# Two-layer diffusion block on one core: seventeen expert loads ahead of the routing, ranks beside the gather, down weights in 8 KB runs

## The chip, the cores and the metric

The kernel runs on one core of a Trainium2 chip. The metric is the device time of one execution in microseconds, as the median of several runs; lower is better. TensorE is called PE here (its weight loads PEld), VectorE DVE, ScalarE ACT, GpSimd POOL, and SyncE SP. SP computes nothing: it issues the loads from device memory (HBM) into the on-chip memory, in the order of its program.

## The reference

Two layers work on 256 latent tokens of width 1024. The first mixes by pooling and latent attention and has a dense SwiGLU. The second mixes by a Hyena convolution and then has a mixture of eight experts of hidden width 3584, of which each token takes two. Everything is float32. The change lies at and behind the routing of the second layer, which is this:

```python
def moe_swiglu(h, router_w, wg, wu, wd):
    t = h.reshape(-1, shp[-1])
    logits = (t @ router_w).astype(jnp.float32)
    top_v, top_i = lax.top_k(logits, TOP_K)
    gates = jax.nn.softmax(top_v, axis=-1)
    combine = jnp.sum(jax.nn.one_hot(top_i, N_EXPERTS) * gates[..., None], axis=1)
    out = jnp.zeros_like(t)
    for e in range(N_EXPERTS):
        out = out + combine[:, e:e + 1] * swiglu(t, wg[e], wu[e], wd[e])

def swiglu(h, wg, wu, wd):
    return (jax.nn.silu(h @ wg) * (h @ wu)) @ wd
```

The weights of all eight experts are read once: 3 x 8 x 1024 x 3584 numbers of 4 bytes, 352 MB.

## The kernel before

**The stages.** Layer one, then the Hyena mixer, whose last step is the output product with `hy_out_w` (keys `ho`, four row blocks). Then come the residual and layer norm of each half of the tokens (tb 0 and 1), the router's logits, and the routing on DVE: `top` twice, a one-hot `mask` of the two experts of each token, and on PE a product with a triangular matrix that gives each token its place among its expert's tokens (`posm`). Then the tokens of expert 0 are gathered by matmuls with one-hot matrices (`gather_open`, `gather_block`), and the experts run.

**The experts.** Slot 0 is expert 0; the other slots are the experts in the order of their token counts, which `weights()` computes on DVE (`key`, `rank`, `pick`, `ids`, and by them `poss` and `combs`). So an address of slot 1 to 7 is known only when SP has read the number from `ids` (`expert`, L179). Slots 0 to 4 have room for 96 tokens (three strips of 32; called H here), slots 5 to 7 for 64 (L). A strip of 32 tokens is the stationary operand, so one expert matmul (L1329) multiplies 32 columns by 256 and four of them share the array. Each slot's 3584 hidden features are cut into four tiles of 1024, 1024, 1024 and 512 (`TILES`); slot and tile make a step, and `STEPS` orders the 32 steps as HH LHHLH LHHLH ... HLHHL.

**A step.** Step i does `up` (gate and up products), `hidden` (silu and product), then the `down` of step i-1, then `turn`: the hidden block, 256 features wide, is transposed by PE in two halves of 128, features 0 to 127 and 128 to 255. In steps 0 and 1 the gather of the next unit of slots follows.

**The loads.** Every expert load is 1 MB in one of a set of 8 KB-per-partition buffers. A step of 1024 features has eight gate and up loads and four down loads, one of 512 features four and two; in all 336 loads, which are numbered from 0 here. A gate or up load is 256 rows by 1024 columns, so runs of 4 KB (2 KB in tiles of 512). A down load is 256 full rows of 4 KB; partition p gets rows p and p + 128 (`"(k p) n -> p k n"`). Loads 0 to 19 are of expert 0 and need no number.

**The buffers.** `wp` holds four `raw`, three `whi` and three `wlo` buffers, which the earlier stages use too: the `ho` rows are split into `whi` and `wlo` parts. When the pools of the Hyena stage close, `mr` (five) and `mt` (two) open in their place. `W(key)` issues the loads up to `depth` ahead of the one asked for. Before the routing it is called with depth NRAW + 1 = 5, when only the four `raw` buffers are there, so load 4 takes the buffer of load 0; then with depth 17. `mt` goes after step 0, so that 15 buffers turn round from then on. `load` chains each load behind the one before; the read of a number at L179 is not in that chain.

**Around it.** `sub_lo(nl, ...)` on POOL makes the low part of the normed tokens. `busy` gives PE idle transposes, 8 and 24 of them, behind each half's logits. `gather_block` takes its result out by ACT and DVE in turn. `carry` (four POOL operations on `h`) waits for `st["late"]`, a small copy behind the last block of the gather.

Of the kernel before, what the change touches and what calls it, by code (L numbers as in the profile page):

```python
# [8 lines left out]
F32 = mybir.dt.float32  # L9
# [8 lines left out]
P = 128  # L18
T = 256
# [41 lines left out]
def block_kernel(ctx: ExitStack, tc: tile.TileContext, A, dbg=None):  # L61
# [50 lines left out]
    def fetch(i):  # L112
        e = plan[i]
        if callable(e[0]):
            e[0] = e[0]().rearrange("(k p) n -> p k n", p=P)
        if e[2] == "place":
            load(e[1]() if callable(e[1]) else e[1], e[0])
            return
        k = e[0].shape[1]
        r = raw_tile(e[4])[:, :k * e[1]].rearrange("p (k n) -> p k n", k=k)  # L120
        load(r, e[0])
        e[3] = r
# [51 lines left out]
    def expert(nm, e):  # L174

        if e == 0:
            return A[nm][0, 0]
        if e not in number:
            number[e] = nc.values_load(st["ids"][0:1, e:e + 1], engines=(mybir.EngineType.SP,), min_val=0, max_val=NE - 1)  # L179
        return A[nm][0][bass.ds(number[e], 1)].rearrange("a k f -> (a k) f")  # L180
# [79 lines left out]
    def want_rest():  # L260
# [34 lines left out]
        def rows_of(nm, e, r, n, c0, w):  # L295

            return lambda: expert(nm, e)[r:r + n, c0:c0 + w]

# [654 lines left out]
    with ExitStack() as ctx2:  # L953
# [89 lines left out]
        with tc.tile_pool(name="hy", bufs=1) as hy:  # L1043
# [126 lines left out]
            dump("mh", yh.bitcast(F32))  # L1170
            st["ahead"], st["depth"] = 0, NRAW + 1
            out_rows(ys, [("ho", r) for r in (2, 3)], [pairs(yh, yl, r) for r in (2, 3)], False, True)
# [8 lines left out]
        mt = late.enter_context(tc.tile_pool(name="mt", bufs=1, side="right"))  # L1181
        extra["me"] = [[(mt, NMT, "raw"), (mr, NME, "raw"), (wp, NRAW, "raw"), (wp, NHL, "whi"), (wp, NHL, "wlo")], -1]
        st["depth"] = NRAW + NME + NMT + 2 * NHL
# [18 lines left out]
        with tc.high_priority():  # L1202
            for tb in range(2):
                residual(ln, ys, t, gates[1, 2], tb)
                for i in range(2):
                    ps = bank()
                    with tc.issue_after(st["out"].ins):
                        for j in range(4):
                            k = 4 * i + j
                            PE.transpose(ps[:, j * P:(j + 1) * P], t[:, tb, k * P:(k + 1) * P], ident)  # L1210
                    zcopy = S.copy(zT[:, tb, 4 * i:4 * i + 4, :], ps.rearrange("p (j n) -> p j n", j=4))
                pl = bank()[:, :NE]
                for k in range(KB):
                    last = PE.matmul(pl, zT[:, tb, k, :], arw[:, k, :], start=k == 0, stop=k == 7)
                sums.append((pl,) + norm(t, tb, h))
                busy((8, 24)[tb], last)
            for tb in range(2):
# [3 lines left out]
                with tc.issue_after(sums[1][3].ins):  # L1221
                    V.tensor_scalar(nr, r, -1.0, None, op0=ALU.mult)
                    V.scalar_tensor_tensor(u, rsum[:, 0, :], m, pl, op0=ALU.mult, op1=ALU.subtract)
                    V.scalar_tensor_tensor(lg[:, tb, :], u, nr, rsum[:, 1, :], op0=ALU.mult, op1=ALU.add)
        st["first"] = st["stat"]
        for tb in range(2):
            with tc.issue_after(zcopy.ins):
                S.copy(nh[:, tb, :], h[:, tb, :])
            st["late"] = sub_lo(nl[:, tb, :], h[:, tb, :], nh[:, tb, :], G)

# [24 lines left out]
        top(lg2, m2, i2, oh2)  # L1255
        st["next"] = V.tensor_tensor(mask, oh1, oh2, op=ALU.add)
        pq = bank()[:, :24]
        pp_ = pq[:, :16].rearrange("p (b e) -> p b e", e=NE)
        tri = cst[:, C_TRI:C_TRI + P]
        PE.matmul(pp_[:, 0, :], tri, mask[:, 0, :], start=True, stop=True)  # L1260
        PE.matmul(pp_[:, 1, :], tri, mask[:, 1, :], start=True, stop=False)
        PE.matmul(pp_[:, 1, :], cst[:, C_ONE:C_ONE + P], mask[:, 0, :], start=False, stop=True)
        V.scalar_tensor_tensor(posm, pp_, 1.0, mask, op0=ALU.add, op1=ALU.mult)
        st["ahead"], st["cut"] = 1, 2
        W(("mg", 0, 0, 0))
# [8 lines left out]
    with tc.tile_pool(name="my", bufs=1) as my, tc.tile_pool(name="me", bufs=1) as me, late:  # L1274
# [100 lines left out]
        def turn(e, f, hid):  # L1375

            hT = []
            for s, t in enumerate(hid):
                n = t.shape[0]
                ps = mbank("ms")[:, :256].rearrange("p (q n) -> p q n", q=2)  # L1380
                for q in range(2):
                    PE.transpose(ps[:, q, :n], t[:, q * P:(q + 1) * P], ident[:n, :n])  # L1382
                x = me.tile([P, 2, P], F32, tag="hT", name="hT", bufs=8)
# [68 lines left out]

        V.tensor_tensor(ex, m2, m1, op=ALU.subtract)
        S.activation(ex, ex, AF.Exp)
        gather_open(0, posm)
        ring = extra["me"]
        for k in range(KB):
            gather_block(0, k, k % 2 == 0)
        done = small.tile([P, 1], F32, tag="done", name="done", bufs=1)
        st["late"] = G.tensor_copy(done, unit[0][1][:, KB - 1, 0:1])  # L1460
        carry(h, g, b)


# [7 lines left out]
        pick, prod = sm([NE, NE], "pick"), sm([NE, NE], "prod")  # L1471
        more = sm([2, NE], "more", I32)

        def by_rank(dst, x):

            V.tensor_tensor(prod, pick, x.unsqueeze(1).to_broadcast(wide), op=ALU.mult)
            V.tensor_reduce(dst, prod, axis=AX.X, op=ALU.add)

        def weights():

            V.tensor_scalar(r1, ex, 1.0, None, op0=ALU.add)
            V.reciprocal(r1, r1)
# [3 lines left out]
            V.tensor_tensor(comb, oh1, oh2, op=ALU.add)  # L1486
            pc = mbank("ms")[:, :NE]
            for tb in range(2):
                PE.matmul(pc, ones, mask[:, tb, :], start=tb == 0, stop=tb == 1)
            V.scalar_tensor_tensor(key, pc, float(-NE), iota8, op0=ALU.mult, op1=ALU.add)  # L1490
            V.memset(key[:, 0:1], -1e6)
            V.tensor_tensor(prod, key.unsqueeze(2).to_broadcast(wide), key.unsqueeze(1).to_broadcast(wide), op=ALU.is_gt)
            V.tensor_reduce(rank, prod, axis=AX.X, op=ALU.add)
            V.tensor_scalar(rank, rank, float(-NE), None, op0=ALU.add)
            V.tensor_tensor(pick, iota8.unsqueeze(2).to_broadcast(wide), rank.unsqueeze(1).to_broadcast(wide), op=ALU.is_equal)
            idf = sm([NE], "idf")
            st["ids"] = sm([NE], "ids", I32)
            by_rank(idf, iota8)
            V.tensor_scalar(st["ids"], idf, float(NE), None, op0=ALU.add)
            for tb in range(2):  # L1500
                by_rank(poss[:, tb, :], posm[:, tb, :])
                by_rank(combs[:, tb, :], comb[:, tb, :])
# [6 lines left out]
            mosti = small.tile([P, 1], I32, tag="r_mosti", name="mosti", bufs=1)  # L1509
            V.tensor_tensor(idf, pc, slots, op=ALU.subtract)  # L1510
            V.tensor_reduce(most, idf, axis=AX.X, op=ALU.max)
# [4 lines left out]
            dump("posm", posm)  # L1516
            return mosti

        NF2 = len(TILES)
# [110 lines left out]
        load(lnb, A["ln_b"][1, 1:2, :].to_broadcast([P, D]))  # L1630
        v = nc.values_load(mosti[0:1, 0:1], min_val=0, max_val=T)
        for n in range(2):
# [111 lines left out]
```

## Time and profile before

| what | us |
|---|---|
| median of three runs (lowest, highest) | 1488.97 (1487.72, 1490.21) |
| the profiled execution, its own time | 1491.33 |
| its span, first to last instruction | 1489.6 |
| PE busy | 1395.9 |
| DVE busy | 532.5 |
| ACT busy | 318.6 |
| POOL busy | 74.6 |
| DMA traffic | 485.88 MB |

The busy time of PE counts overlapping matmuls that wait for one another as busy, so it doesn't tell how much faster PE could go; the distance from one group of matmuls to the next does. The page cuts the span into 40 slices of 37.2 us and gives for each the rate of the DMA engines in GB/s.

### The profile page before, as it was taken

The numbers are of one execution on the slowest core, as the hardware profiler recorded it, in microseconds if no ns is written. First come the engines' busy times: TensorE is split into PE (matmuls) and PEld (weight loads), VectorE is DVE, ScalarE is ACT, GpSimd is POOL, SyncE is SP. The second block draws the span as 40 slices with busy tenths as digits, with TensorE's granted clock in tenths as the row PEclk, the third lists the DMA queues.
The fourth block names the chain that finished last, engine by engine and source line by source line (L and its number), as shares of the span: only waits on it lengthen the run. The fifth ranks groups of instructions, "written<-read, shape, count | busy, mean of one in ns | idle before, by whom it ended". The sixth has DMA issues, their size and how long they took to land. (4 is left out here: it accounts for less than half of the span.)

```text
span 1489.6 us, 39345 instructions
## 1 busy us (share of the span) xinstructions
PE 1395.9 (94%) x17906; PEld 943.1 (63%) x17907; DVE 532.5 (36%) x889; ACT 318.6 (21%) x515; POOL 74.6 (5%) x68
## 2 busy tenths in 40 slices
PE   6899998999989997999999999999899999999994
PEld 3676778999979885565555555555465555455552
DVE  5656788886588765100110002200002110110005
ACT  2546643334344430100000011000010000000000
POOL 1300011000020203000000000000000000000000
PEclk9999998999999997999999999999999999999997
DMA  9965798897562622999999999999999999999992
GB/s 295 327 233 170 258 351 292 299 312 268 184 201 69 237 89 109 408 408 401 407 407 408 407 390 407 408 408 407 399 387 400 408 407 384 408 408 408 389 389 99
DMA packets 179888, 485.88 MB, mean 326 GB/s; under 512 B 8829, under 2 KB 49981, under 8 KB 179645
## 3 DMA queue, kind: packets, MB, share of 16 engines
q1 hardware_dynamic: 178112, 479.97, 84.9%
q10 hardware_dynamic: 1598, 3.27, 0.7%
q8 instruction: 144, 2.36, 0.7%
q14 instruction: 34, 0.28, 0.1%
HBM read 480.06 MB, written 3.15 MB: 324 GB/s over the span
## 5 line engine op out<-in xcount | busy, mean ns | idle before, releaser
L1329 PE MATMUL up<-raw,xt 128*32 128x256 f32 x9408 | 536.7, 382 | 21.4 <-DMA raw<-in_moe_gate_dram 11.0
L1329 PEld LDWEIGHTS up<-raw,xt 128*32 128x32 f32 x9408 | 303.5, 110 | 236.7 <-DMA raw<-in_moe_up_dram 20.0
L1366 DVE TENSOR_TENSOR sg<-up,sg 128x256 f32<-128x256 f32 (+1 forms) x71 | 30.0, 423 | 545.8 <-ACT sg L1364 545.5
L1329 PE MATMUL ac<-raw,hT 128*32 128x256 f32 x3360 | 192.0, 380 | 0.5 <-DMA raw<-in_moe_down_dram 0.5
L160 PE MATMUL mm<-zl,whi 128*128 128x256 f32 x544 | 155.5, 286 | 4.3 <-DVE zl L164 4.3
L159 PE MATMUL mm<-zh,whi 128*128 128x256 f32 x544 | 155.7, 289 | 1.0 <-DVE m L1106 1.0
L135 DVE TENSOR_TENSOR wlo<-raw,whi 128x2048 fp32r<-128x2048 f32 (+4 forms) x63 | 137.9, 2192 | 51.4 <-ACT whi L131 51.3
L161 PE MATMUL mm<-zh,wlo 128*128 128x256 f32 x544 | 153.5, 284 | 0.0
L1329 PEld LDWEIGHTS ac<-raw,hT 128*32 128x32 f32 x3360 | 107.6, 110 | 72.1 <-issue 2.7
L1364 ACT ACTIVATE sg<-up 128x256 f32<-128x256 f32 (+1 forms) x76 | 28.6, 382 | 576.2 <-PE up L1329 574.3
L131 ACT CAST whi<-raw 128x2048 fp32r<-128x2048 f32 (+3 forms) x61 | 113.1, 1854 | 151.7 <-PE mm L160 84.7
L160 PEld LDWEIGHTS mm<-zl,whi 128*128 128x128 f32 x544 | 104.8, 193 | 7.4 <-DVE zl L164 5.9
L159 PEld LDWEIGHTS mm<-zh,whi 128*128 128x128 f32 x544 | 104.3, 193 | 4.3 <-ACT zh L887 1.7
L161 PEld LDWEIGHTS mm<-zh,wlo 128*128 128x128 f32 x544 | 104.4, 192 | 0.5 <-issue 0.5
L1329 PE MATMUL al<-raw,hT 128*32 128x256 f32 x1344 | 80.7, 381 | 3.0 <-DVE hT L1387 2.1
L842 POOL TENSOR_TENSOR v<-v,mhalf 128x1 f32<-128x1 f32 x8 | 6.3, 793 | 1221.1 <-DVE v L841 1221.1
L1329 PEld LDWEIGHTS al<-raw,hT 128*32 128x32 f32 x1344 | 42.7, 110 | 31.2 <-issue 3.2
L1387 DVE COPY hT<-ms 128x256 f32<-128x256 f32 (+1 forms) x47 | 19.6, 417 | 112.8 <-PE ms L1382 111.1
L419 DVE SCALAR_TENSOR_TENSOR part<-raw,sS,part 128x512 f32<-128x512 f32 x56 | 50.0, 892 | 1.3
L1451 DVE SCALAR_TENSOR_TENSOR h<-ms,combs,h 128x512 f32<-128x512 f32 x32 | 23.2, 748 | 70.6 <-PE ms L1450 70.5
L1382 PEld LDWEIGHTS ms<-cst,sg 128*128 128x128 f32 (+1 forms) x152 | 16.0, 140 | 31.0 <-DVE sg L1366 15.6
L1382 PE MATMUL ms<-cst,sg 128*128 128x128 f32 (+1 forms) x152 | 30.3, 292 | 5.4 <-DVE sg L1366 4.2
(349 smaller groups left out, 1476.0 us busy)
## 6 DMA issues: line engine op xcount, KB each, us to landing
raw<-in_moe_gate_dram SPq DMA_DIRECT2D x112, 1024.0 KB, 18.4
raw<-in_moe_up_dram SPq DMA_DIRECT2D x112, 1024.0 KB, 18.5
raw<-in_moe_down_dram SPq DMA_DIRECT2D x112, 1024.0 KB, 18.5
raw<-in_ada_w_dram SPq DMA_DIRECT2D x48, 1024.0 KB, 6.3
raw<-in_hy_in_w_dram SPq DMA_DIRECT2D x12, 1024.0 KB, 5.6
raw<-in_ffn_gate_dram SPq DMA_DIRECT2D x11, 1024.0 KB, 8.2
raw<-in_ffn_up_dram SPq DMA_DIRECT2D x11, 1024.0 KB, 8.2
raw<-in_ffn_down_dram SPq DMA_DIRECT2D x11, 1024.0 KB, 6.9
```

What stands on the lines that cost most here:

```text
L131: S.copy(hi, r)
L135: V.tensor_tensor(lo[:, ks, :], r[:, ks, :], hi[:, ks, :].bitcast(F32), op=ALU.subtract)
L159: PE.matmul(out, lh, rh, start=start, stop=False)
L160: PE.matmul(out, lh, rl, start=False, stop=False)
L161: return PE.matmul(out, ll, rh, start=False, stop=stop)
L419: V.scalar_tensor_tensor(acc, w[:, k, :], s, acc, op0=ALU.mult, op1=ALU.add)
L1329: PE.matmul(out[32 * G:32 * G + 32, :], lhs[G], rhs[G], start=start, stop=stop, tile_position=(0, 32 * G))
L1364: S.activation(t, ps[s][:rows, :256], AF.Silu)
L1366: V.tensor_tensor(t, ps[s][:rows, 256:512], t, op=ALU.mult)
L1382: PE.transpose(ps[:, q, :n], t[:, q * P:(q + 1) * P], ident[:n, :n])
L1387: V.tensor_copy(x[:, :, :n], ps[:, :, :n])
L1451: V.scalar_tensor_tensor(h[:, tb, cs], ps, weight(tb), h[:, tb, cs], op0=ALU.mult, op1=ALU.add)
```

## The change

Five things change.

- The ring of buffers is turned: before the routing only four loads are asked for, one for each `raw` buffer; then the next thirteen go to `mt`, `mr`, `whi` and `wlo`, and `raw` comes last. The reads of expert numbers (and the read of `mosti` at the end) are chained behind the last load.
- Down loads take `"(p k) n -> p k n"`: partition p gets rows 2p and 2p + 1, one run of 8 KB. `turn` transposes the even and the odd features of the block apart, so the operand is read with a step of two.
- The ranks: `ranks()` is split from `weights()` and issued right behind the gather's matmuls; the count of tokens per expert is multiplied on PE beside the positions. `done` on POOL now also waits for `poss`, and `carry` behind it. The softmax of the two logits (`ex`) moves into `weights()`.
- The gather is taken out by ACT alone.
- `nh` of each half is cast on ACT right behind that half's logits; `nl` is made on DVE, the first half between the two halves' logits, the second behind `mask`. The 8 idle transposes of the first half go.

```diff
@@ fetch, expert, rows_of
-            e[0] = e[0]().rearrange("(k p) n -> p k n", p=P)
+            e[0] = e[0]()
...
-            number[e] = nc.values_load(st["ids"][0:1, e:e + 1], engines=(mybir.EngineType.SP,), min_val=0, max_val=NE - 1)
+            with tc.issue_after(st["last"].ins):
+                number[e] = nc.values_load(st["ids"][0:1, e:e + 1], engines=(mybir.EngineType.SP,), min_val=0, max_val=NE - 1)
...
-            return lambda: expert(nm, e)[r:r + n, c0:c0 + w]
+            how = "(p k) n -> p k n" if nm == "moe_down" else "(k p) n -> p k n"
+            return lambda: expert(nm, e)[r:r + n, c0:c0 + w].rearrange(how, p=P)
@@ ahead of the routing
-            st["ahead"], st["depth"] = 0, NRAW + 1
+            st["ahead"], st["depth"] = 0, NRAW
...
-        extra["me"] = [[(mt, NMT, "raw"), (mr, NME, "raw"), (wp, NRAW, "raw"), (wp, NHL, "whi"), (wp, NHL, "wlo")], -1]
+        extra["me"] = [[(mt, NMT, "raw"), (mr, NME, "raw"), (wp, NHL, "whi"), (wp, NHL, "wlo"), (wp, NRAW, "raw")], -1]
@@ the routing
-                busy((8, 24)[tb], last)
+                with tc.issue_after(zcopy.ins):
+                    S.copy(nh[:, tb, :], h[:, tb, :])
+                if tb:
+                    busy(24, last)
...
+                    if tb == 0:
+                        sub_lo(nl[:, 0, :], h[:, 0, :], nh[:, 0, :])
         st["first"] = st["stat"]
-        for tb in range(2):
-            with tc.issue_after(zcopy.ins):
-                S.copy(nh[:, tb, :], h[:, tb, :])
-            st["late"] = sub_lo(nl[:, tb, :], h[:, tb, :], nh[:, tb, :], G)
...
         st["next"] = V.tensor_tensor(mask, oh1, oh2, op=ALU.add)
+        with behind("next"):
+            sub_lo(nl[:, 1, :], h[:, 1, :], nh[:, 1, :])
...
+        for tb in range(2):
+            PE.matmul(pq[:, 16:], ones, mask[:, tb, :], start=tb == 0, stop=tb == 1)
         V.scalar_tensor_tensor(posm, pp_, 1.0, mask, op0=ALU.add, op1=ALU.mult)
+        count = eq[:, 0, :]
@@ turn
-                    PE.transpose(ps[:, q, :n], t[:, q * P:(q + 1) * P], ident[:n, :n])
+                    PE.transpose(ps[:, q, :n], t.rearrange("p (n q) -> p q n", q=2)[:, q, :], ident[:n, :n])
@@ the gather and the ranks
-        V.tensor_tensor(ex, m2, m1, op=ALU.subtract)
-        S.activation(ex, ex, AF.Exp)
-        gather_open(0, posm)
-        ring = extra["me"]
-        for k in range(KB):
-            gather_block(0, k, k % 2 == 0)
-        done = small.tile([P, 1], F32, tag="done", name="done", bufs=1)
-        st["late"] = G.tensor_copy(done, unit[0][1][:, KB - 1, 0:1])
-        carry(h, g, b)
...
+        def ranks():
+
+            V.scalar_tensor_tensor(key, count, float(-NE), iota8, op0=ALU.mult, op1=ALU.add)
...
+            by_rank(idf, iota8)
+            last = V.tensor_scalar(st["ids"], idf, float(NE), None, op0=ALU.add)
+            for tb in range(2):
+                by_rank(poss[:, tb, :], posm[:, tb, :])
+            return last
...
+        gather_open(0, posm)
+        V.tensor_copy(count, pq[:, 16:])
+        ring = extra["me"]
+        for k in range(KB):
+            gather_block(0, k)
+        last = ranks()
+        st["late"] = last
+        done = small.tile([P, 1], F32, tag="done", name="done", bufs=1)
+        st["late"] = G.tensor_tensor(done, unit[0][1][:, KB - 1, 0:1], poss[:, 1, 0:1], op=ALU.mult)
+        carry(h, g, b)
@@ the end
-        v = nc.values_load(mosti[0:1, 0:1], min_val=0, max_val=T)
+        with tc.issue_after(st["last"].ins):
+            v = nc.values_load(mosti[0:1, 0:1], min_val=0, max_val=T)
```

## Rows read from the trace of the kernel before

**Rows 1.** Page, 40 slices of the span: DMA rate in GB/s

```profile
GB/s 295 327 233 170 258 351 292 299 312 268 184 201 69 237 89 109 408 408 401 407 407 408 407 390 407 408 408 407 399 387 400 408 407 384 408 408 408 389 389 99
```

**Rows 2.** Windows in and behind the gather: busy us by engine, PE clock, DMA share, GB/s

```profile
565.00:568.00 3.00, 2.47 (x12) 2.50 (x12) 1.69 (x10) 0.43 (x1) 0.00 (x0) 0.50 0.00 0
577.00:581.00 4.00, 4.00 (x84) 2.21 (x76) 3.93 (x3) 0.00 (x0) 4.00 (x3) 1.00 0.00 0
```

**Rows 3.** Timeline of SP: start us, us, queue, line, load

```profile
534.93 0.37 SPq L106 DMA_DIRECT2D raw<-in_moe_up_dram  x1
584.26 0.37 SPq L106 DMA_DIRECT2D raw<-in_moe_gate_dram  x1
```

**Rows 4.** Waits of SP, 500 to 600 us: total, times, longest

```profile
SPq L179 <- DVE ids L1499: 47.9, 1, 47.9
```

**Rows 5.** DMA view, windows 195:200, 1440:1443, 600:605, 500:505 us: packets, MB, rate

```profile
DMA packets 1725, 1.74 MB, mean 348 GB/s; under 512 B 25, under 2 KB 1725, under 8 KB 1725
...
DMA packets 576, 1.15 MB, mean 384 GB/s; under 512 B 16, under 2 KB 16, under 8 KB 576
...
DMA packets 529, 2.04 MB, mean 408 GB/s; under 512 B 31, under 2 KB 31, under 8 KB 529
...
DMA packets 462, 1.76 MB, mean 352 GB/s; under 512 B 32, under 2 KB 32, under 8 KB 462
```

**Rows 6.** Timeline of PE later: step 5, step 14, step 30

```profile
729.79 1.93 PE L1329 MATMUL up<-raw,xt 128*32 128x256 f32 x32 [0.63 <-DMA raw<-in_moe_up_dram]
...
966.69 20.90 PE L1329 MATMUL up<-raw,xt 128*32 128x256 f32 x384
...
1422.90 11.59 PE L1329 MATMUL up<-raw,xt 128*32 128x256 f32 x177 [1.45 <-DMA raw<-in_moe_up_dram]
```

**Rows 7.** Groups by line and form: busy us, mean ns, idle before; from 573 us

```profile
L1329 PE MATMUL up<-raw,xt 128*32 128x256 f32 x9408 | 536.7, 382 | 21.4 <-DMA raw<-in_moe_gate_dram 11.0 <-DMA raw<-in_moe_up_dram 10.3
L1329 PE MATMUL ac<-raw,hT 128*32 128x256 f32 x3360 | 192.0, 380 | 0.5 <-DMA raw<-in_moe_down_dram 0.5
L1329 PE MATMUL al<-raw,hT 128*32 128x256 f32 x1344 | 80.7, 381 | 3.0 <-DVE hT L1387 2.1 <-DMA raw<-in_moe_down_dram 0.8
L1382 PE MATMUL ms<-cst,sg 128*128 128x128 f32 x132 | 27.4, 297 | 5.4 <-DVE sg L1366 4.2 <-DVE hT L1387 0.3
```

**Rows 8.** Timeline of PE around and in steps 0 and 1

```profile
549.26 0.40 PE L161 MATMUL acc<-whi,yl 128*128 128x512 f32 x1
...
573.28 12.16 PE L1329 MATMUL up<-raw,xt 128*32 128x256 f32 x192
589.29 12.25 PE L1329 MATMUL up<-raw,xt 128*32 128x256 f32 x192 [3.85 <-DMA raw<-in_moe_gate_dram]
...
606.31 20.27 PE L1329 MATMUL up<-raw,xt 128*32 128x256 f32 x371
...
626.43 10.73 PE L1329 MATMUL ac<-raw,hT 128*32 128x256 f32 x191
...
641.05 13.80 PE L1329 MATMUL up<-raw,xt 128*32 128x256 f32 x251
```

**Rows 9.** Timeline of DVE, routing and ranks

```profile
556.38 4.43 DVE L1224 SCALAR_TENSOR_TENSOR lg<-u,nr,rsum 128x8 f32<-128x8 f32 x2
...
563.12 0.17 DVE L1256 TENSOR_TENSOR mask<-oh,oh 128x16 f32<-128x16 f32 x1
564.90 0.18 DVE L1263 SCALAR_TENSOR_TENSOR posm<-mm,mask 128x16 f32<-128x16 f32 x1 [1.61 <-PE mm L1262]
...
573.71 1.98 DVE L1492 TENSOR_TENSOR prod<-key 128x64 f32<-128x64 f32 x1
...
583.05 0.22 DVE L1476 TENSOR_TENSOR prod<-pick,posm 128x64 f32<-128x64 f32 x1
```

**Rows 10.** Timeline of POOL, same stretch

```profile
556.11 4.67 POOL L164 TENSOR_TENSOR nl<-h,nh 128x1024 fp32r<-128x1024 f32 x2 [2.60 <-ACT nh L1228]
```

**Rows 11.** Groups by line and form, weight loads of `turn`, 600 to 1480 us

```profile
L1382 PEld LDWEIGHTS ms<-cst,sg 128*128 128x128 f32 x132 | 14.1, 140 | 28.9 <-DVE sg L1366 15.6 <-issue 11.9 <-DVE hT L1387 0.9
```

More of the change, by code (lines that the diff above doesn't have):

```diff
@@ L1472, in block_kernel @@
         more = sm([2, NE], "more", I32)
+        idf = sm([NE], "idf")
         def by_rank(dst, x):
@@ L1477, in by_rank @@
             V.tensor_reduce(dst, prod, axis=AX.X, op=ALU.add)
+        def ranks():
+            V.scalar_tensor_tensor(key, count, float(-NE), iota8, op0=ALU.mult, op1=ALU.add)
+            V.memset(key[:, 0:1], -1e6)
+            V.tensor_tensor(prod, key.unsqueeze(2).to_broadcast(wide), key.unsqueeze(1).to_broadcast(wide), op=ALU.is_gt)
+            V.tensor_reduce(rank, prod, axis=AX.X, op=ALU.add)
+            V.tensor_scalar(rank, rank, float(-NE), None, op0=ALU.add)
+            V.tensor_tensor(pick, iota8.unsqueeze(2).to_broadcast(wide), rank.unsqueeze(1).to_broadcast(wide), op=ALU.is_equal)
+            st["ids"] = sm([NE], "ids", I32)
+            by_rank(idf, iota8)
[3 more added lines that the diff above has]
+            return last
         def weights():
+            V.tensor_tensor(ex, m2, m1, op=ALU.subtract)
+            S.activation(ex, ex, AF.Exp)
             V.tensor_scalar(r1, ex, 1.0, None, op0=ALU.add)
@@ L1486, in weights @@
             V.tensor_tensor(comb, oh1, oh2, op=ALU.add)
-            pc = mbank("ms")[:, :NE]
             for tb in range(2):
[L1489 to L1501, printed above, removed]
                 by_rank(combs[:, tb, :], comb[:, tb, :])
@@ L1509, in weights @@
             mosti = small.tile([P, 1], I32, tag="r_mosti", name="mosti", bufs=1)
-            V.tensor_tensor(idf, pc, slots, op=ALU.subtract)
+            V.tensor_tensor(idf, count, slots, op=ALU.subtract)
             V.tensor_reduce(most, idf, axis=AX.X, op=ALU.max)
```

## The prediction

> **What bounds the kernel now.** I read the page's slices first: from slice 17 on, where the experts run, the DMA rate is 384 to 408 GB/s, and ahead of them it is low: 69, 237, 89, 109 [rows 1]. The windows of the gather show a hole: from 565 to 568 us no byte moves [rows 2]. SP's timeline says why: the last early load goes out at 534.9, the next (load 4) at 584.3 [rows 3], and in between SP waits 47.9 us for `ids` [rows 4]. The read of an expert's number stands ahead of loads that need no number.
>
> Once the experts run, DMA is the bound. A load of 1.0486 MB at 408 GB/s [rows 5] takes 2.57 us. Where PE needs less, its groups of 32 matmuls take 1.93 us and it then waits, 0.63 us in the row shown, together 2.56: DMA's pace [rows 6]. Such waits before `up` sum to 21.4 us [rows 7], and they go on to step 30, where PE still waits 1.45 us [rows 6]. From that wait, at 1422.9, the rest (down of step 29, step 31, the last scatter, norm, store) is 1489.6 - 1422.9 = 66.7 us of work of PE and DVE, which I leave as it is.
>
> PE is a close second. Freely fed it spaces matmuls at 20.9 / 384 = 54.4 ns [rows 6]. So an H load (48 matmuls) takes PE 2.61 us and an L load (32) 1.74 us, against 2.57 for DMA.
>
> **The lead, step by step.** After the change loads 0 to 3 go out as now. Loads 4 to 10 need `mt` and `mr`, whose place is free when the Hyena pools close; their last reader is done before the `ho` product's last rows, and I take 540. Loads 11 to 16 need `whi` and `wlo`, which the `ho` product reads until 549.7 [rows 8]. Seven loads of 2.57 us from 540 keep DMA busy until 558, so the later six come in time. Thirteen loads end at 540 + 13 x 2.57 = 573.4. Load 17 takes the buffer of load 0, for which PE needs 2.6 us, and follows at once if PE begins by 570.8.
>
> When does PE begin? Now at 573.3 [rows 8]. The chain in front of it gets shorter:
> - The second half's logits stand 4.43 us on DVE for two operations of about 0.2 us each, from 556.4 to 560.8, exactly as long as POOL's `nl` runs (4.67 us from 556.1) [rows 9, 10]. With `nl` off POOL this goes; one `nl` half comes in on DVE, about 1.2 us as an estimate (no row shows it there; bounds 0.7 and the 2.3 it takes on POOL). Without the 8 idle transposes the second half's logits come up to 0.8 us earlier. Net about 4 us.
> - The second `nl` half lies behind `mask`, beside PE's position matmuls, for which DVE waits 1.61 us anyway [rows 9]. The cover is thin; if it is gone, 1.2 us.
> - The count matmuls move from behind the gather to beside the positions: 0.9 us saved behind, 0 to 0.9 us spent before.
>
> So PE begins 4 to 5 us earlier. The gather ran at half clock (0.50) after PE had stood still for `mask`; at 577 the clock is 1.00 [rows 2]. With that gap closed it may stay at 1.00, worth up to 2 us more. ACT alone must then empty eight blocks, some 0.6 us each, no longer than PE's pace of 0.85 a block at half clock. I take 568.5 for PE's start, between 566 and 570.
>
> So DMA no longer stops. By loads alone, load 17 starts at 573.4. Now load 4 starts at 584.3, so load 17 at 584.3 + 13 x 2.57 = 617.7: **44.3 us earlier**.
>
> **What is given back.** Only 15 buffers turn round. Load 35 needs the buffer of load 20, the first of step 2. Steps 0 and 1 are both H, and PE sets their pace: up 20.9 (freely fed), transposes and gather to the next up 4.7, up 20.1, down 10.6, transposes and gather 4.0, together 60.3 us, and 1.7 us for load 20 itself [rows 6, 8]. From 568.5 this is 630.5. DMA alone would be there at 573.4 + 18 x 2.57 = 619.7, so 10.8 us are lost. Now load 35 starts at 584.3 + 31 x 2.57 = 664.0. **Net 33.5 us.** From step 2 on the L steps free buffers faster than DMA fills them, and DMA sets the pace again to the end. In this sum a microsecond of PE's start is a microsecond of the end.
>
> **The runs of 8 KB.** A third of the traffic, 112 loads. At a full DMA the spacing of packets on each of 16 engines is, from the counts less those under 512 B, 47.1 ns for 1 KB, 85.7 for 2 KB, 160.6 for 4 KB [rows 5]. That is nearly a line: 37.8 ns per KB and 9.5 ns per packet. Half the packets of a load (128 of 256) on 16 engines save 128 x 9.5 / 16 = 76 ns, **8.5 us** in all. Bounds: 0, if a run is cut at 4 KB, to about 17 (twice the fit, as no row shows 8 KB).
>
> The Trainium skill ("DMA: Bandwidth & Descriptors", Why small descriptors are slow) gives a fixed overhead of about 3 cycles per packet, at 32 bytes a cycle. By that, as an estimate, 8 KB in one packet saves 3 of 262 cycles, 0.03 us per load, 3.3 us in all, and the sum would be 5 us shorter. The rows put the overhead per packet at two to three times that, and I go by the rows.
>
> **Edits at no cost.** The ranks run on DVE while PE and ACT gather. Their operations of 2 us become 0.2 us, as the same kind of operation shows later [rows 9], because `carry` on POOL now waits for `poss`. So `ids` come about 565, before load 20 goes out. SP's read stands behind load 19 then; were `ids` late, all loads from 20 on would stand behind it, 1 us for 1 us. `carry` and the softmax (with its table load on ACT) move behind the gather and beside step 0's 25 us; who needs them is the first scatter, over 100 us later. The read of `mosti` behind the last load: 0 to 2 us at the end; I take 0.
>
> **The strided transposes.** 152 weight loads (132 and 20 of a second form) of 140 ns [rows 11] now read with a step of two. The trace has no strided weight load. Bounds: nothing, or doubled: 152 x 0.14 = 21 us of PE's time. DMA bounds most steps, so I take 0 and keep the rest for the range. For PE meeting its own bound in pairs of H steps (two take it 2 x (31.3 + 1.4) = 65.4 us against 24 x 2.57 = 61.7) I take 2 us.
>
> **Sum.** 33.5 + 8.5 - 2 = 40 us off 1491.3, the profiled execution: 1451.3. The median of the runs is 2.4 us lower, so **1449**.
>
> **Rivals.**
> - PE becomes the bound. Its own work is (9408 + 3360 + 1344) x 54.4 ns = 768 us, and the other groups of that view (the transposes' 27.4 is the largest [rows 7]) sum to 90, overlaps counted. From 568.5 this ends at 1426; now PE ends at about 1476. So 50 us of gain are left at the least, more than DMA's 42; with 21 us of slower weight loads 29, so 1460. For it: the lead takes away the waits in which PE's spare time lies. Against it: every L step has 10 us to spare. Chance 0.17.
> - The change doesn't do what it says: the thirteen loads still wait, for a buffer or for `ids`. Then only the earlier `ids` count: load 4 at about 566 in place of 584.3 gives 18, the runs 8.5, so 1462. Against it: thirteen separate buffers, and the read is chained behind the loads. Chance 0.07.
> - More: PE starts at 566 at full clock, and the 8 KB runs give twice the fit: 33.5 + 2.5 + 17 = 53, so 1436. Chance 0.11.
> - Slower: long contiguous runs stream worse. The `ho` loads, whole rows of 4 KB, show 352 GB/s in one window [rows 5]. At that rate a down load takes 2.98 us, 0.41 more, 46 us in all: 46 - 33.5 = 12.5 slower, 1501. It decides from 0.30 us per down load on. Against it: down loads are whole rows already and run at 408. Chance 0.05.
>
> **How the numbers follow.** My forecast has 0.60. Its own range is 1440 (0.15 us per down load) to 1457 (the runs bring nothing). The range that holds eight in ten takes in PE's bound, the late loads and part of "more": 1437 to 1465. Slower by over 0.2% is the last rival, 0.05; within 0.2%, which is about what a measurement here can tell from no change, 0.02; faster 0.93.
>
> **What would show it.** SP: loads 4 to 16 out by 550 us, and no wait for `ids` over 1 us. Windows from 540 to 570: 400 GB/s where there is nothing. PE's first expert matmul at 566 to 570, and no DMA wait in steps 0 and 1. SP waiting for PE's buffers, some 10 us in all, between 585 and 630. Windows with down loads alone: near 420 GB/s, half the packets. Weight loads of `turn` still at 140 ns. Step 30 still waiting for its load, some 42 us earlier. I am wrong if the hole only moves to where buffers are missing, if PE shows no waits for DMA any more, or if down loads land no faster.

## The result and the profile after

| | median us (lowest, highest) | ratio to before, 95% interval |
|---|---|---|
| before | 1488.80 (1487.72, 1490.21) | |
| after | 1453.93 (1447.97, 1454.99) | 0.9757 (0.9729 to 0.9785) |

The change takes 34.9 us off the median. The profiled execution went from 1491.33 to 1453.02 us, its span from 1489.6 to 1451.3. The forecast was 1449, so 40 us were expected; the time lies in the range. Executions of the changed kernel are up to 7 us apart, and from profile to profile the stages ahead of the experts differ: the same early load of the experts is issued up to 7 us earlier or later (520.2 to 526.9 us). So profiles are compared below from PE's first expert matmul on, and times by medians.

**The hole is gone.** The page's slices of after, DMA rate in GB/s, which answer to [rows 1], with the line of all packets:

```profile
GB/s 303 325 249 176 224 356 297 319 304 276 211 148 145 203 197 396 290 373 406 410 412 411 406 404 409 412 412 411 385 408 404 411 411 387 410 413 412 389 398 79
DMA packets 165553, 485.88 MB, mean 335 GB/s; under 512 B 8830, under 2 KB 49982, under 8 KB 150974
```

Slices 14 and 15 (counted from 0) go from 89 and 109 to 197 and 396: the loads now run beside the routing. Slice 16 goes the other way, from 408 to 290. That is the price, and SP's timeline of after shows it (start, us, queue, line, load), where [rows 3] jumped from 534.93 to 584.26:

```profile
537.95 0.37 SPq L106 DMA_DIRECT2D raw<-in_moe_gate_dram  x1
...
552.27 2.35 SPq L106 DMA_DIRECT2D raw<-in_moe_up_dram  x1
554.66 23.36 SPq L106 DMA_DIRECT2D raw<-in_moe_down_dram  x4
580.28 0.40 SPq L106 DMA_DIRECT2D raw<-in_moe_gate_dram  x1
588.05 0.39 SPq L106 DMA_DIRECT2D raw<-in_moe_up_dram  x1
```

Load 4 goes out at 537.95, load 15 at 552.27. Then the four down loads of step 0 (loads 16 to 19) take until 578, and from 580 on the loads come as PE frees buffers. Waits of SP from 500 to 660 us (total, times, longest):

```profile
SPq L106 <- PE up L1337: 69.0, 23, 16.7
```

The 47.9 us for `ids` [rows 4] are gone; `ids` are written at 562.58, long before load 20, the first that needs them, goes out at 580.28. SP waits for PE instead (the expert matmul, L1329 before, is L1337 now); most of the 69.0 us are covered by loads already on their way. Windows of after: length, busy us of PE, PEld, DVE, ACT and POOL, PE clock, DMA share, GB/s:

```profile
540.00:560.00 20.00, 19.76 (x121) 17.70 (x119) 15.23 (x40) 5.73 (x8) 1.11 (x2) 0.91 1.02 409
580.00:600.00 20.00, 19.68 (x312) 11.58 (x308) 2.80 (x9) 3.45 (x8) 0.00 (x0) 1.00 0.58 207
600.00:620.00 20.00, 20.00 (x380) 12.02 (x376) 1.27 (x3) 1.15 (x3) 0.00 (x0) 1.00 1.01 393
620.00:640.00 20.00, 19.78 (x322) 12.34 (x318) 0.85 (x2) 2.29 (x5) 0.00 (x0) 1.00 0.91 342
640.00:1400.00 760.00, 750.04 (x12820) 443.61 (x12816) 83.87 (x174) 57.27 (x138) 0.00 (x0) 1.00 1.02 406
```

409 GB/s beside the routing, where there was a hole [rows 2]; then a thin stretch between 580 and 640, while PE works through steps 0 and 1; then a full stream to 1400, at 406 GB/s. At that rate the three thin windows lack 20 x (199 + 13 + 64) / 406 = 13.6 us of stream.

**PE starts earlier and never waits for a load.** PE's timeline of after (start, us, engine, line), which answers to [rows 8]:

```profile
567.25 23.32 PE L1337 MATMUL up<-raw,xt 128*32 128x256 f32 x384
595.55 20.27 PE L1337 MATMUL up<-raw,xt 128*32 128x256 f32 x371
...
630.44 13.80 PE L1337 MATMUL up<-raw,xt 128*32 128x256 f32 x251
```

First expert matmul at 567.25 (573.28 before), step 2 at 630.44. All waits of PE from 566 to 1440:

```profile
PE ms L1458 <- ACT yh L1447: 4.0, 4, 2.0
PE ms L1390 <- DVE sg L1374: 3.2, 6, 0.5
PE ms L1458 <- ACTq L1647: 2.1, 1, 2.1
PE al L1337 <- DVE hT L1395: 2.0, 1, 2.0
PE ms L1458 <- DVE h L1459: 1.4, 3, 0.6
PE ms L1458 <- DVE yl L164: 0.8, 1, 0.8
PE ms L1428 <- DVE h L1459: 0.4, 1, 0.4
PE ms L1390 <- DVE hT L1395: 0.3, 1, 0.3
```

14.2 us in all, none for DMA, where 21.4 stood before `up` [rows 7]. The last group that answers to a row of before is the weight load of the transposes in `turn` (L1390), 140 ns in [rows 11] (count, then busy us, mean ns, idle):

```profile
L1390 PEld LDWEIGHTS ms<-cst,sg 128*128 128x128 f32 x132 | 20.5, 205 | 26.9 <-issue 12.3 <-DVE sg L1374 11.1 <-DVE hT L1395 1.7
```

So one thing that I had named as a sign of a wrong forecast is there: PE shows no waits for DMA any more. And two signs that were to bear it out are missing: the weight loads of `turn` are not at 140 ns, and step 30 doesn't wait for its load. The time came near the forecast all the same. What follows asks who sets the pace after the change, and what each part was worth.

### The profile page after: what moved, and what is told of

It is laid out like the page before. It is cut to its first block, busy times and chain, and to the rows that moved or that the text cites. A ratio compares the mean times of both kernels' runs of the same rounds, so it can differ in the third digit from the quotient of the medians.

```text
span 1451.3 us, 39340 instructions
## 1 busy us (share of the span) xinstructions
PE 1387.6 (96%) x17898; PEld 952.9 (66%) x17899; DVE 520.8 (36%) x888; ACT 320.6 (22%) x519; POOL 70.0 (5%) x66
## 5 line engine op out<-in xcount | busy, mean ns | idle before, releaser
L1337 PE MATMUL up<-raw,xt 128*32 128x256 f32 x9408 | 527.7, 382 | 0.0
L1337 PEld LDWEIGHTS up<-raw,xt 128*32 128x32 f32 x9408 | 305.5, 110 | 203.4 <-issue 9.4
L1337 PE MATMUL ac<-raw,hT 128*32 128x256 f32 x3360 | 190.2, 380 | 0.0
L1337 PEld LDWEIGHTS ac<-raw,hT 128*32 128x32 f32 x3360 | 109.6, 110 | 68.5
L1337 PE MATMUL al<-raw,hT 128*32 128x256 f32 x1344 | 78.8, 381 | 2.0 <-DVE hT L1395 2.0
L1337 PEld LDWEIGHTS al<-raw,hT 128*32 128x32 f32 x1344 | 42.2, 110 | 30.1 <-DVE hT L1395 2.2
L1390 PEld LDWEIGHTS ms<-cst,sg 128*128 128x128 f32 (+1 forms) x152 | 23.3, 206 | 29.0 <-issue 14.0
L1393 ACT COPY hT<-ms 128x256 f32<-128x256 f32 (+1 forms) x29 | 10.5, 363 | 137.2 <-PE ms L1390 137.2
```

The lines of the kernel that those rows point to most:

```text
L1337: PE.matmul(out[32 * G:32 * G + 32, :], lhs[G], rhs[G], start=start, stop=stop, tile_position=(0, 32 * G))
L1390: PE.transpose(ps[:, q, :n], t.rearrange("p (n q) -> p q n", q=2)[:, q, :], ident[:n, :n])
```

## The experiments

Three readings were set against each other. **P**: PE sets the end after the change. **D**: the stream of loads does, as in my sum. **B**: the two end within a few microseconds of each other, so that a little taken from one is worth little.

### The parts one by one

**Everything but the runs of 8 KB.** The changed kernel with down loads as before; the transposes are then contiguous too.

```diff
-            how = "(p k) n -> p k n" if nm == "moe_down" else "(k p) n -> p k n"
+            how = "(k p) n -> p k n"
...
-                    PE.transpose(ps[:, q, :n], t.rearrange("p (n q) -> p q n", q=2)[:, q, :], ident[:n, :n])
+                    PE.transpose(ps[:, q, :n], t[:, q * P:(q + 1) * P], ident[:n, :n])
```

> The changed kernel with the down loads back at 4 KB runs (rows p and p + 128) and the transposes without a step; lead and routing stay. Theory P: only the weight loads count, 10 us less, 1443 to 1444. Theory D: 112 loads are 0.05 to 0.076 us longer each, 6 to 8.5 us more, 1459 to 1462. Theory B: PE gets faster, DMA slower and becomes the bound, 1455 to 1458, with waits of PE for DMA late in the run.

1458.33 us (ratio 0.9797, 0.9763 to 0.9831), 30.8 below the kernel before in the same session (1489.12). That lies between the ranges of B and D. By P the contiguous transposes would have gained; the kernel got slower. PE's waits for loads come back (waits of PE, 566 to 1445 us), and over the long window the stream is at 402 GB/s, where the changed kernel has 406:

```profile
PE up L1337 <- DMA raw<-in_moe_up_dram: 3.0, 4, 1.5
PE up L1337 <- DMA raw<-in_moe_gate_dram: 2.6, 3, 1.6
```

```profile
640.00:1400.00 760.00, 743.72 (x12706) 431.77 (x12701) 82.97 (x172) 55.42 (x133) 0.00 (x0) 1.00 1.02 402
```

**The lead alone.** The kernel before with the ring turned, four loads ahead of the routing and the reads chained, and the old routing.

```diff
+            with tc.issue_after(st["last"].ins):
+                number[e] = nc.values_load(st["ids"][0:1, e:e + 1], ...)
...
-            st["ahead"], st["depth"] = 0, NRAW + 1
+            st["ahead"], st["depth"] = 0, NRAW
...
-        extra["me"] = [[(mt, NMT, "raw"), (mr, NME, "raw"), (wp, NRAW, "raw"), (wp, NHL, "whi"), (wp, NHL, "wlo")], -1]
+        extra["me"] = [[(mt, NMT, "raw"), (mr, NME, "raw"), (wp, NHL, "whi"), (wp, NHL, "wlo"), (wp, NRAW, "raw")], -1]
```

> The kernel before with the turned ring, the depth of four, and the reads of numbers chained behind the loads; runs and routing as before. PE begins at 573.3 as before; load 17 goes out about 574 to 576; load 35 at 573.3 + 62 = 635.3 in place of 664.0. Theory D: 28.7 us less than before, about 1460 to 1463. Theory P: PE's own 858 us of work from 573.3 and the 13.6 us behind it, 1446 to 1450.

1463.55 us (0.9833, 0.9806 to 0.986): 25.6 gained, 3 less than the 28.7 of the sum, and just outside the range of theory D; theory P is far off. So the routing, which fills most of the diff, is worth 30.8 - 25.6 = 5.2 us on top, about what PE starts earlier.

**The routing alone.** The kernel before with the new order of routing, ranks and gather; ring, order of loads and down loads as before.

> The kernel before with the new routing, ranks and gather, but the old ring, the depth of five and the unchained reads, 4 KB runs. SP still stands at the read of ids, which come about 562.6 in place of 583, so load 4 goes out about 564 and DMA stands idle from 542 to 564. Theory D: 20 us less than before, 1467 to 1470. Theory P: PE begins at 567.3 and is not held by DMA, 1440 to 1445.

1477.24 us (0.9923, 0.9902 to 0.9944): 11.9 gained, little more than half of what the sum had. SP's waits from 500 to 660 us show one part of why, and its timeline the other:

```profile
SPq L179 <- DVE ids L1487: 28.0, 1, 28.0
```

```profile
531.99 0.37 SPq L106 DMA_DIRECT2D raw<-in_moe_up_dram  x1
570.10 0.37 SPq L106 DMA_DIRECT2D raw<-in_moe_gate_dram  x1
```

The wait for `ids` shrinks from 47.9 to 28.0 us and is over near 560, yet load 4 goes out only at 570.10. In the old ring load 4 takes the buffer of load 0, which PE has to read first, and PE's first expert matmul is at 564.7. A second lock stood right behind the first and couldn't be seen in the kernel before, because the first one opened later.

**The runs of 8 KB alone**, in the kernel before: the down loads and the strided transposes of the change, nothing else.

> The kernel before with only the down loads in 8 KB runs and the transposes with a step of two; ring, reads and routing as before. DMA is the bound there (PE waits 21 us for it), and in the changed kernel packets of 8 KB are 315 to 317 ns apart, 416 GB/s against 408: 0.05 us per load. Theory D: 112 x 0.05 = 5.6 us less, up to the 8.5 of the prediction, 1480 to 1484; PE's 10 us of slower weight loads vanish in its waits. Theory P: 10 us more, 1499.

1482.16 us over ten executions (0.995, 0.9935 to 0.9965): 6.5 gained, between 5.2 and 9.7 by the interval. PE still waits 16.3 us for loads before `up`. What the strided transposes cost here was not measured apart. The stream over the long window went from 403 to 407 GB/s, before and here:

```profile
640.00:1400.00 760.00, 732.15 (x12429) 420.22 (x12432) 81.12 (x167) 55.23 (x132) 0.00 (x0) 1.00 1.02 403
...
640.00:1400.00 760.00, 738.70 (x12566) 432.59 (x12562) 81.15 (x167) 53.99 (x129) 0.00 (x0) 1.00 1.02 407
```

The rival in which long runs stream worse (1501) is out.

### Who sets the pace

**Less work for PE.** The changed kernel without the last 128 of the 1024 rows of each gate and up product (its output lacks their share); all loads stay.

```diff
                         k = q * per + j
+                        if k == KB - 1:
+                            continue
```

> The changed kernel without the last of the eight 128-row blocks of the gate and up products: 1176 of PE's 9408 up matmuls are left out, all loads stay. PE's work in the experts falls by 1176 x 54.4 ns = 64 us. Theory P: 1390. Theory D or B: DMA's line is left standing; it ends where the sum of the prediction puts it, less what PE holds back in steps 0 and 1 (about 5 us there), 1442 to 1449, and PE waits for DMA for most of the 64 us.

1442.47 us over two executions (0.9686, 0.9653 to 0.9719). 64 us of PE's work are gone and 11.5 us of time. The stream doesn't notice (window, columns as above), and PE's waits for it are back (waits of PE, 566 to 1440 us):

```profile
640.00:1400.00 760.00, 711.12 (x11802) 409.88 (x11790) 82.79 (x173) 57.19 (x138) 0.00 (x0) 0.99 1.02 406
```

```profile
PE up L1337 <- DMA raw<-in_moe_up_dram: 20.3, 22, 1.7
PE up L1337 <- DMA raw<-in_moe_gate_dram: 9.0, 13, 1.7
```

406 GB/s, as in the changed kernel. Most of what it gains lies at the two ends: the thin stretch (568 to 640: 347 GB/s against 323) and PE's shorter remainder behind the last load.

**Less for DMA.** The changed kernel with half of each down load, which is multiplied in both places (its output is that of other weights); PE's work stays.

```diff
+            if nm == "moe_down":
+                n = n // 2
...
-    [w[:, j, o * 256:(o + 1) * 256] for i, o in does]
+    [w[:, 0, o * 256:(o + 1) * 256] for i, o in does]
```

> The changed kernel with only the first 128 rows of each down load read (half a megabyte, runs of 4 KB) and multiplied twice, in place of 256: DMA's work falls by 112 x 1.25 = 140 us, PE's stays. Theory D: at least 40 us less, 1410 or below. Theory P or B: PE's line is left standing, 1448 to 1454, as before this edit within 5 us, and DMA stands idle in between.

1438.13 us over two executions (0.9657, 0.9622 to 0.9691). Some 140 us of stream are gone (58.7 MB at 411 GB/s) and 15.8 us of time. So D in its strict form is out, and the time came out below what P and B had as well. PE hardly stands still any more, in the same window:

```profile
640.00:1400.00 760.00, 759.68 (x13085) 451.66 (x13077) 84.49 (x176) 57.26 (x139) 0.00 (x0) 1.00 0.92 342
```

From the first expert matmul to the last scatter matmul takes 858.0 us here, 860.7 with less PE work, 870.4 in the changed kernel. So with either side relieved the stage ends 10 to 12 us earlier. One caution: in both of these kernels PE's instructions of this stage came out in another order than in the changed kernel, so more than the one thing differs. Here PE's waits for DVE and ACT are 5.3 us and not 14.2, and those 8.9 us are most of the 12.4.

**Contiguous transposes with 8 KB runs** (the packed kernel). In the changed kernel ACT and DVE write the hidden block with even and odd features apart, so that PE reads it without a step.

```diff
-                S.activation(t, ps[s][:rows, :256], AF.Silu)
+                S.activation(apart(t), ps[s][:rows, :256].rearrange("p (n q) -> p q n", q=2), AF.Silu)
...
-                    PE.transpose(ps[:, q, :n], t.rearrange("p (n q) -> p q n", q=2)[:, q, :], ident[:n, :n])
+                    PE.transpose(ps[:, q, :n], t[:, q * P:(q + 1) * P], ident[:n, :n])
```

> The changed kernel, but ACT and DVE write the hidden block with its even and odd features already apart, so that PE's 152 weight loads of the transposes read without a step. In the changed kernel these loads take 205 ns in place of 140 and PE shows no wait for DMA. Theory P (PE sets the end from its first expert matmul on): 152 x 0.065 = 10 us less, 1443 to 1444. Theory D (DMA sets the pace, as the sum of the prediction had it): no change, 1451 to 1454. Theory B (both lines end within some 5 us of each other): about half of it comes through, 1447 to 1450, and PE waits for DMA again.

1449.94 us (0.9749, 0.9725 to 0.9773), in the range of B. The weight loads are back at 140 ns (groups of PEld, from 560 us):

```profile
L1393 PEld LDWEIGHTS ms<-cst,sg 128*128 128x128 f32 x132 | 14.1, 140 | 27.8 <-DVE sg L1377 12.5 <-issue 12.4 <-DVE hT L1398 1.8
```

But this profile's expert stage is no shorter (885.0 us from the first expert matmul to the span's end, 884.05 in the changed kernel); its start was merely early. So both were measured again on one chip:

> The changed kernel again, beside the packed one on the same chip, to measure the step of two in the weight loads of the transposes. Near 1453. Theory 1 (PE sets the end, and the slower weight loads are on its path): 3 to 10 us above the packed kernel. Theory 2 (loads set the end): no more than 1 us above it.

> The packed kernel again, same chip. Theory 1: 1443 to 1450, 3 to 10 us below the changed kernel. Theory 2: 1452 to 1453, as the changed kernel. From the two profiles at hand, where the packed kernel comes to step 30 2.8 us sooner and then waits 1.0 us for its load: 2 to 3 us below, 1450.

1452.66 against 1451.36 us. Over both sessions, nine executions each, the means are 1452.9 and 1450.3: 2.6 us for the step of two, with an error of about 1.2: between the two theories, and not clear of zero by much. That is far from the 10 us that 152 loads of 65 ns more sum to.

**The transposes held back.** The packed kernel with the transposes of a step behind the last down matmul of that step, so that PE isn't made to ask for a hidden block in the middle of the down product.

```diff
                 for q in range(2):
-                    PE.transpose(ps[:, q, :n], t[:, q * P:(q + 1) * P], ident[:n, :n])
+                    with behind("down"):
+                        PE.transpose(ps[:, q, :n], t[:, q * P:(q + 1) * P], ident[:n, :n])
```

> The changed kernel with the hidden block written with even and odd features apart, and the transposes of a step held behind the last down matmul of that step, so that PE is not made to ask for a hidden block in the middle of the down product. In the changed kernel's profile PE stands 14.2 us in the expert stage for results of DVE and ACT, in the run with half the down bytes, whose instruction order is another, 5.3. Theory 1 (those standstills set the end): some 5 to 9 us less than the packed kernel, 1441 to 1445. Theory 2 (the stream of loads is only some 3 us ahead of PE and sets the end as soon as PE is quicker): within 2 us of the packed kernel, 1448 to 1452, and PE then shows waits for DMA of several us. Theory 3 (the transposes come later than the next step wants them): slower than the packed kernel by 2 to 6 us.

1450.42 us (0.9738, 0.9718 to 0.9757): the same as the packed kernel, theory 2. Waits of PE in this kernel, 566 to 1440 us, those over 1 us:

```profile
PE up L1337 <- DMA raw<-in_moe_up_dram: 4.2, 6, 1.1
PE al L1337 <- DMA raw<-in_moe_down_dram: 2.6, 6, 0.5
PE al L1337 <- DVE hT L1396: 2.1, 1, 2.1
PE ms L1459 <- ACTq L1649: 2.1, 1, 2.1
PE ms L1391 <- DVE hT L1396: 1.8, 6, 0.3
PE ac L1337 <- DMA raw<-in_moe_down_dram: 1.2, 2, 0.7
PE up L1337 <- DMA raw<-in_moe_gate_dram: 1.2, 1, 1.2
```

PE's waits for ACT's `yh` are gone, and 9.2 us of waits for DMA have taken their place, in nearly the same time. From the first expert matmul to the last scatter matmul it is 867.3 us, 3.1 less than the 870.4 of the changed kernel, which shows no wait for DMA. But 1.3 of the 3.1 are PE's clock and not the loads. The first group of step 0, against 23.32 us above, is:

```profile
567.29 22.00 PE L1337 MATMUL up<-raw,xt 128*32 128x256 f32 x384
```

From 567 to 577 us the granted clock is 0.87 here and 0.74 in the changed kernel. So the loads allow about 867.3 + 1.3 = 868.6 (an estimate), and PE in the changed kernel ends some 2 us behind that. The two profiles of the packed kernel, 871.5 and 868.3, lie 3 us apart. That is B: the two lines end within a few microseconds of each other. That PE ends last in the changed kernel rests on its showing no wait for a load; 2 us are too few to be shown by one profile of each. Of the 12.4 us by which the run with less DMA is shorter, the waits for DVE and ACT explain 8.9; 3.5 are left that no row names.

### The clock in the gather

The packed kernel with the eight idle transposes of the first half's logits back, to see whether the gather then runs at the full clock.

```diff
-                if tb:
-                    busy(24, last)
+                busy((8, 24)[tb], last)
```

> The packed kernel (hidden block written with even and odd features apart) with the eight idle transposes of the first half put back. In the changed kernel PE's clock falls to 0.50 at about 555 us, before the mask, and is back at 1.00 only at 572: gather 6.4 us, first up 23.3. In the kernel before it held 1.00 until 562. If the eight transposes hold it over the shorter gap, gather and first up take some 4 us less and the end comes 3 to 4 us earlier, 1446. If the clock falls all the same, the transposes cost up to 0.8 us, 1451.

1449.94 us, nothing gained. Windows of this kernel, whose first expert matmul is at 566.5:

```profile
553.00:556.00 3.00, 3.00 (x30) 3.00 (x28) 2.54 (x12) 2.73 (x3) 0.00 (x0) 1.00 1.03 410
556.00:559.00 3.00, 2.51 (x23) 2.30 (x22) 2.73 (x12) 0.29 (x2) 0.00 (x0) 1.00 1.02 406
559.00:562.00 3.00, 2.21 (x16) 2.02 (x15) 2.60 (x21) 0.83 (x2) 0.00 (x0) 0.87 1.03 411
562.00:568.00 6.00, 6.00 (x38) 5.21 (x41) 2.57 (x16) 3.52 (x7) 0.82 (x2) 0.50 1.02 409
568.00:574.00 6.00, 6.00 (x88) 2.97 (x80) 0.00 (x0) 0.35 (x1) 6.00 (x3) 0.71 0.93 337
```

The clock stays at its upper level until about 561.2, 5 us ahead of the first expert matmul, and then is at half all the same, through the gather and into step 0. In these windows PE stands still for under 1 us in three, ahead of the fall.

## Why the prediction held, and where it didn't

**The lead** (44.3 us): right. Load 4 went out 46.3 us earlier, 2 us more than I took. The thirteen loads filled 540 to 560 at 409 GB/s.

**PE's start** (568.5): right, 567.25. The routing's steps came as worked out: the `nl` half on DVE takes 1.22 us (estimated 1.2). The hope of a full clock in the gather was not fulfilled, and it costs more than the gather: step 0's `up` takes 23.3 us, not the 20.9 of a freely fed one. So step 2 begins at 630.44, not at 628.8.

**The give-back** (10.8): the mechanism is right and a little larger, 13.6 us of lost stream: 2 more because the stream ran that much earlier into the same wall, and 1.6 because PE was later at step 2 (together 14.4). Only the second is lost to the time. Net 33.5 - 1.6 = 31.9, and the kernel with everything but the 8 KB runs measured 30.8. The lead alone fell 3 us short of its sum; why was not found.

**The runs of 8 KB** (8.5): right, as far as the times tell. The clean pair is the kernel with 4 KB runs and the packed one, both with contiguous transposes and of one session, which otherwise differ only in how ACT and DVE write the hidden block: 1458.33 against 1449.94, 8.4 us (7.8 by the means of all their executions, with an error of 2.1). In the kernel before they gave 6.5. (The changed kernel itself is 4.4 us below the one with 4 KB runs, but it also pays for the step of two.) The long windows agree: the 352 MB take 876 us at 402 GB/s and 868 at 406, some 8 us less, give or take 2 for the rounding of the rates. The spacing of packets that I worked from gives less. I drew a line through packets of 1, 2 and 4 KB and took 9.5 ns for each packet saved. After the change, windows in which nearly all packets are of 8 KB show (DMA view, 672 to 676 and 728 to 732 us):

```profile
DMA packets 231, 1.66 MB, mean 416 GB/s; under 512 B 28, under 2 KB 28, under 8 KB 28
...
DMA packets 226, 1.66 MB, mean 416 GB/s; under 512 B 24, under 2 KB 24, under 8 KB 24
```

Without the short ones that is 64 us / 203 = 315 and 64 / 202 = 317 ns per packet, against 2 x 160.6 = 321.2 for two of 4 KB: 4.4 to 5.9 ns saved, so 35 to 47 ns per load, and 4 to 5 us over 112 loads. These are windows of 4 and 5 us; the window of 760 us weighs more.

The Trainium skill ("DMA: Bandwidth & Descriptors", Why small descriptors are slow), with its fixed overhead of about 3 cycles per packet, gave an estimate of 3.3 us; the measured 6.5 to 8.4 lie nearer to the 8.5 of my fit.

**The strided transposes** (0, bounds 0 to 21): the loads did get slower, 140 to 205 ns, which is 10 us over 152. Only 2.6 (error 1.2) reach the time, but I had put them at 0, since the loads were to set the pace. A matmul of `turn` has a mean of 327 ns with the step and 297 without, so about half of the longer load lies beside other work of PE. The Trainium skill ("TensorE: Matmul & The Clock Gate", Step-by-step: what each phase is for) says that the next weights load while the current matmul runs; the 30 of 65 ns agree in part.

**PE meeting its own bound** (2 us off): it can't be told apart from the strided loads. From kernel to kernel the medians give 30.8 for lead and routing, 8.4 for the runs and 4.0 back for the step of two (2.6 by the means), in all 35.2; the table above has 34.9. The forecast had 33.5, 8.5 and 2 back, 40. So what it lacked is 2.7 us of the lead and about 2 of the strided transposes, each hardly more than the error of a run.

**DMA to the end.** This step is not borne out. The sum let the loads set the end, with step 30 still waiting for its load. After the change PE waits for no load, at step 30 or elsewhere, and ends some 2 us behind what the loads allow, as far as single profiles tell. So the rival "PE becomes the bound" is nearly what the profile shows, and I had named its sign as one of a wrong forecast. PE's own work I had nearly right: 768 + 90 = 858 us from its start; without the waits listed it is 870.4 - 14.2 = 856.2 in the changed kernel and 858.0 - 5.3 = 852.7 in the run with less DMA. But its end (1426) left out the 14.2 us of waits for DVE and ACT. With them PE's line would have given 50 - 14.2 = 36 us of gain, less than the 42 of the loads, and PE would have been the bound of the sum. That the time is so near the forecast is in part luck: the two lines end close together, so that the sum over the loads gave nearly the right time though PE ends no earlier.

**The loads still wait** (1462): not so here, but the routing alone shows that I had mis-sized it. With the old ring only 11.9 us come from earlier `ids` and an earlier start of PE, not 18, since load 0's buffer is the next lock.

## What to carry to other kernels

Loads that stand behind a run-time number should be sorted by what they wait for: those that need neither the number nor a buffer still in use go first, and the next lock behind the one removed must be named before the gain is counted. Where an engine's waits for loads vanish, the margin to the next bound is not yet known: look at the rate of the other resource over the whole stretch, and take some work off each side in turn. Where two resources end within about a per cent of each other, what is taken from one comes back only in small part: here 11.5 us of 64 from PE, 15.8 of 140 from the loads.

## What the runs showed of the chip

- A weight load of 128 x 128 in float32 takes 140 ns with contiguous columns and 205 ns with a step of two; the matmul behind it shows 30 ns of the 65.
- In windows of 4 us, packets of 8 KB take 315 to 317 ns on one of the 16 engines, 416 GB/s in all; 4 KB showed 160.6 ns and 408 GB/s in one of 5 us. Over 760 us, with a third of the loads in 8 KB runs and not 4, the stream went from 402 to 406 and, in the kernel before, from 403 to 407 GB/s. The 6.5 to 8.4 us that this gave are 2 to 3% of the 288 us that those loads take.
- PE's granted clock was at 0.50 through most of the gather in every kernel here, also where only 0.5 to 0.8 us of each 3 before the fall were idle, as in the one with eight more transposes. In the changed kernel it also fell at about 555, though the profile has PE busy for all 3 us from 553 to 556 (clock 0.85 in that window). What would hold it at its upper level was not found.
